# A two-layer attention step on one core: a share of background work at every step, the scale chain issued in pieces, and weights split two jobs ahead

## The chip, the core and the metric

The kernel runs on one core of a Trainium2 chip. The engines are TensorE (PE in the profile, its weight loads PEld), VectorE (DVE), ScalarE (ACT), GpSimd (POOL), and SyncE (SP), from whose queue all the transfers here are issued. The metric is the device time of one execution in microseconds (us), as the median of several runs. Before the change it is 2208.05 us (three runs, 2207.29 to 2210.84).

## The reference

A step of a streaming encoder with two layers, on 2048 prompt frames and 64 sample frames of width 1024. Both layers have the same form and different attention:

```python
def project(x, norm_g, w_in, q_g, k_g, n_heads, n_kv):
    h = rms_norm(x, norm_g)
    p = h @ w_in
    q, k, v, gate = jnp.split(p, [wq, wq + wkv, wq + 2 * wkv], axis=-1)
    q = rms_norm(q.reshape(*lead, n_heads, HEAD_DIM), q_g)
    k = rms_norm(k.reshape(*lead, n_kv, HEAD_DIM), k_g)
...
def gated_attention_layer(...):
    qp, kp, vp, gp = project(x_p, norm_g, w_in, q_g, k_g, n_heads, n_kv)
    op = prompt_band_attention(qp, kp, vp, past_chunks, bias_fn, sinks)
    y_p = x_p + (op * jax.nn.silu(gp)) @ w_out
    ...
```

Layer A has 16 query heads on 2 key heads of 64, a window of the own 64-frame chunk and two before it, a position bias and a sink per head. Layer B has 16 heads with their own keys and values, the own chunk and eight before it, and a bias by clipped distance. The sample frames attend to a cache and to themselves. The outputs are y for both streams and the newest rows of keys and values of both layers. All inputs are float32.

## The kernel before

**Numbers.** Matrix products keep nearly float32 precision by splitting each operand into a high part and a low rest: a projection is three matmuls (high by high, high by low, low by high: lines 679 to 681). In layer B both parts are float16, so the weights are first scaled by a power of two, found on the chip from the largest weight.

**Tiling.** The prompt is cut into eight units of 256 frames (u0 to u7, two tiles of 128 each); the 64 sample frames are a ninth unit. They are worked in the order u0 to u6, sample, u7. Layer A takes four passes of four heads over all units; layer B takes eight passes, each over one pair of heads (`hp` 0 to 7). Between and after them stand the output projections, in blocks of 264 frames.

**Two streams on PE.** Only PE's order is written out by hand. A `Filler` holds all projection jobs of the whole kernel in a list (a job is one unit of one pass) and hands out pieces of them: `filler.to(mark)` steps through generators until so much projection work (counted in us) is done. The attention of layer B (`pipeline` in `layer_b`) goes through the units; a unit has four steps, y = 0 to 3 (two tiles by two heads). Each step issues the score matmuls and the softmax of its tile and head (`scores`), a share of background work, some filler, then what has become due from earlier steps (`due`: the transposes of the probabilities, called `values`, and the products with V), and more filler up to the step's goal. At the end of step 1 the queries and keys of the next unit are transposed (`queries`). For passes after the first, the probabilities of the pair's first head are transposed by DMA instead (`TURNED`), so that two of the four steps have no `values`. In these passes the filler is half a unit ahead of the attention.

**Background work.** Small work on the other engines that isn't bound to a place is put in a queue (`Background`) with a cost in us: head norms (0.6 and 0.4, urgent), gates (0.3), the low parts of queries and keys (`low`, two of 1.0 each, urgent), weight splits (0.66). `bg.share(BL, BP_, KC)` takes from it up to a budget of 1.8 or a quarter of what is queued, whichever is more, and one weight split (two, when more than eight are left). An item issued so comes, on its engine, behind the last softmax instructions issued before it (`anchor`). What isn't taken in time is issued where it is first needed. Within these ties the order on DVE, ACT, POOL and SP is set at build time by a scheduler that goes by the order of issue and by estimates of durations.

**Weights of layer B.** A pass needs eight chunks of 128 x 512 weights, each loaded (line 445), scaled and split into two float16 parts: ACT makes the high part (line 467), DVE the rest (line 470). There are twelve buffers for split chunks (`WN`); a pass holds eight, so four of the next pass can be split early, the others only when the last job of the pass (u7) frees its buffers. `Filler.step` calls for the weights at the start of a job: all of them when the pass begins one job later, and the first four when it begins three jobs later (`EARLY`).

**The scale chain.** `scale_work` runs after each projected tile of layer B, counted by `at` (twice the unit plus the tile). For the next pass it loads the weights once more in chunks (`scan`, line 182), reduces each to its largest value on DVE (line 175, `most`), combines them (`input_top`), turns the column into a row with a PE transpose into the PSUM tile tp and forms a power of two in a few one-element DVE instructions (`input_across`, lines 197 to 208), and spreads it over the partitions with a matmul into tp, a copy to `scl` (lines 212, 213) and a multiplication with the gains, `gsb` (`input_scales`, line 230). The ACT splits read `gsb`. There is one buffer of tp; the transposes of `queries` use it too, and `low` (lines 1367 and 1371) is its last reader. The score matmuls (lines 1416, 1417) and the transposes of probabilities (line 844) share two buffers of the PSUM tile sb, which the softmax pass (line 1420) or the probability splits (lines 816, 817) free.

Of the kernel before, what the change touches and what calls it, by code (L numbers as in the profile page):

```python
# [34 lines left out]
WB = 3  # L35
XB = 4
XN = 7
EARLY = 3
MORE = 4.7
WN = 12  # L40
AVG_A = 5.02
# [7 lines left out]
QY = 1  # L49
# [7 lines left out]
def hybrid_encoder_kernel(  # L57
# [76 lines left out]
    held = {}  # L134
# [85 lines left out]
    def input_across(h):  # L220
        across(h, h + 1)
        e, r, o = row[:, 16:17], row[:, 17:18], row[:, 20:23]
        powers(row[:, h : h + 1], e, r)
        times(o[:, 0:1], r, WB_)
        times(o[:, 1:2], e, 1 / (HB * WB_))
        times(o[:, 2:3], e, 0.5 / VB if h > 0 and len(TURNED) == 2 else 0.5 / (VB * PB))

    def input_scales(h):
        everywhere(h, row[:, 20:23])
        nc.vector.tensor_scalar(gsb[:, h], gain[:, 1, :], S_W(h), 1.0, op0=ALU.mult, op1=ALU.mult)  # L230
# [25 lines left out]
    def scale_work(hp, u, e):  # L256
        at = 2 * u + e
        if hp < 7:
            if at < 8:
                scan(8 * (hp + 1) + at)  # L260
            elif at == 8:
                scan()
                input_top(hp + 1)
            elif at == 10:
                input_across(hp + 1)
            elif at == 11:
                input_scales(hp + 1)
            i = 64 + 3 * hp + (at - 11)
            if 11 <= at < 14 and i < 84:
                scan(i)  # L270
            elif at == 14:
                scan()
        elif u == 0:
            (output_top, output_across)[e]()
        elif at == 2:
            output_scales()
# [585 lines left out]
        return Q2[turn[0] % 2]  # L862


    class Filler:
        def __init__(self):
            self.jobs, self.n, self.gen, self.done, self.total = [], -1, None, 0.0, 0.0
            self.attending = False

        def add(self, prefetch, weights, gen, early=True):  # L870
            j = Item()
            j.prefetch, j.weights, j.gen, j.early = prefetch, weights, gen, early
            self.jobs.append(j)

        def step(self):
            if self.gen is None:
                self.n += 1
                if self.n >= len(self.jobs):
                    return False
                if self.n == 0:  # L880
                    self.x = self.jobs[0].prefetch()
                    self.jobs[0].weights()
                for q in self.x.items:
                    bg.run(q)
                if self.n + 1 < len(self.jobs):
                    nxt = self.jobs[self.n + 1]
                    self.x = nxt.prefetch()
                    if nxt.weights is not None:
                        nxt.weights()
                if self.n + EARLY < len(self.jobs):  # L890
                    nxt = self.jobs[self.n + EARLY]
                    if nxt.weights is not None and nxt.early:
                        nxt.weights(WN - 8)
                self.gen = self.jobs[self.n].gen()
            c = next(self.gen, None)
            if c is None:
                self.gen = None
                return self.step()
            self.done += c
            if not self.attending:  # L900
                bg.drain(FR * c)
            return True
# [5 lines left out]
    filler = Filler()  # L908
    finished = {}

    def layer_a():
# [4 lines left out]
        def add_unit(qd, place, unit):  # L916
            u, T, tiles = unit
# [116 lines left out]
                mine[0].mark = filler.total  # L1034
            if qd == 0 and unit is order[-1]:
                mine[0].mark += 8 * 3 * 256 / 2400
            filler.add(prefetch, weights if place == 0 else None, first if qd == 0 and u == 0 else gen, qd > 1)

        for qd in range(4):
            for place, unit in enumerate(order[2:5] + order[:2] + order[5:] if qd == 1 else order):  # L1040
# [215 lines left out]
    def layer_b():  # L1256
# [4 lines left out]
        def add_unit(hp, unit):  # L1261
            u, T, tiles = unit
            it = Item()
            it.hp, it.unit, it.ready = hp, unit, False
            its.append(it)
            last = u == NU
            cols = slice(2 * hp * HD, (2 * hp + 2) * HD)

            def prefetch():
                for j in range(NO):  # L1270
                    assert finished["x1", j] == 2 or j * OT >= u * UT + T
                rows = None if hp else token_rows(unit)
                st.x[hp, u] = x = load_act(
                    x1, u * UT, T, False, T == TS, None, xs[1], hp > 0, F16, rows
                )
                return x

            def weights(*m):
                if hp not in st.emit:
                    (st.w[hp],), _, st.emit[hp] = load_weights(1, (w_in_b[hp], 512), scale=gsb[:, hp])  # L1280
                st.emit[hp](*m)

            def gen():
                xc = st.x.pop((hp, u))
                it.prs, it.todo = [], []
                it.gate = t("pb", [P, 2, P], 5)
                if "VH" not in held:
                    held["VH"], held["two"] = (
                        x.rearrange("p (a b c) -> p a b c", b=2, c=P)
                        for x in split_at(t("values", [P, 4 * NT * P], 1, F16), 2 * NT * P)  # L1290
                    )
                    held["turn"] = 0
                for e, (tt, t0, n) in enumerate(tiles):
                    out = []
                    c = yield from project((tt, t0, n), xc, st.w[hp], 512, out)
                    if last:
                        pr, sums = evacuate_sample(hp, out[0], it.gate[:, e])
                        it.prs.append(pr)
                        v, kn = pr[:n, 256:384], pr[n:, 0:128]
                        it.todo += [sums] + head_norm(P, pr[:, 0:128]) + gate(P, it.gate[:, e, 0:HD])  # L1300
                        it.todo.append(
                            store_kv(1, slice(n, P), kn, v, kb_s[192:256, cols], vb_s[192:256, cols])
                        )
                        it.ready = True
                        yield c
                        continue
                    pr = evacuate_b(hp, tt, out[0], it.gate[:, e])
                    it.prs.append(pr)
                    v, kn = pr[:n, 256:384], pr[:n, 128:256]
                    it.todo += head_norm(n, pr[:n, 0:256]) + gate(n, it.gate[:n, e])  # L1310
                    if it is its[0] and e == 0:
                        block_scales(TOK - OT)
                    if tt >= NT - 4:
                        o = (tt - (NT - 4)) * P
                        it.todo.append(
                            store_kv(1, slice(0, P), kn, v, kb_p[o : o + P, cols], vb_p[o : o + P, cols])
                        )
                    it.ready = e == len(tiles) - 1
                    scale_work(hp, u, e)
                    yield c  # L1320

            filler.total += 8 * (6 if T == UT else 2) * 512 / 2400
            it.mark = filler.total
            filler.add(prefetch, weights if u == 0 else None, gen)

        for hp in range(8):
            for unit in order:
# [307 lines left out]
        def pipeline():  # L1635
# [12 lines left out]
            def due(at):  # L1648
                flush()
                now = [x for x in todo if x[0] <= at]  # L1650
                todo[:] = [x for x in todo if x[0] > at]
                short, rests, vals = [], [], []
                for _, kind, x in now:
                    if kind == "products":
                        between, rest = products(*x)
                        short += between
                        rests.append(rest)
                    else:
                        {"values": vals, "call": rests}[kind].append(x)
                for x in vals:  # L1660
                    values(*x, short)
                    bg.share(BL, BP_, KC)
                for fn in short + rests:
                    fn()

            for x, it in enumerate(its):
# [13 lines left out]
                for y, (i, h) in enumerate(heads):  # L1680
                    scores(it, i, h)
                    bg.share(BL, BP_, KC)
                    goal(2 * y + 1)
                    due(step)
                    todo += [(step + d, kind, o) for d, kind, o in then(it, i, h)]
                    step += 1
                    if sample and x + 1 < len(its):
                        queries(its[x + 1])
                        flush()
                        near = 1e9  # L1690
                    goal(2 * y + 2)
                    if not sample and y == QY and x + 1 < len(its):
                        queries(its[x + 1])
                        near = 1e9
# [234 lines left out]
```

## Time and profile before

| what | value |
|---|---|
| median of three runs | 2208.05 us (2207.29 to 2210.84) |
| the profiled execution | 2212.35 us, span 2210.5 us |
| PE busy | 2110.9 us, 95% |
| DVE busy | 1547.2 us, 70% |
| ACT busy | 1424.8 us, 64% |
| POOL busy | 999.5 us, 45% |
| mean granted TensorE clock | 0.987 |
| moved by DMA | 372.87 MB, mean 169 GB/s |

The span runs from the first to the last instruction of the profiled execution. Busy times are shares of it by engine; matmuls overlap, so the busy time of PE says how long it had work, not how well it used it. Idle time is told by what ended it: a line "PE sb L1416 <- ACT gt L1237" says that PE's instruction of line 1416, which writes tile sb, waited for ACT's instruction of line 1237, which writes gt. Layer B's attention takes the span from about 880 to 2040 us, the last output projection the rest.

### The profile page before, as it was taken

How to read it: one execution, taken by the hardware profiler on the slowest of the kernel's cores; microseconds unless marked ns; L12 is line 12 of the kernel's file. 1: busy time of each engine (PE TensorE's matmuls, PEld its weight loads, DVE VectorE, ACT ScalarE, POOL GpSimd, SP SyncE). 2: the span in 40 equal slices, each digit the busy share in tenths (PEclk: the TensorE clock that was granted, in tenths of full speed). 3: DMA queues.
4: the chain of work that ended last, by engine and by line, in shares of the span. 5: the costliest groups of instructions: out<-in, count | busy, mean ns of one | idle time of the engine just before them, and what ended most of it. 6: DMA issues, size and time to landing. Idle time of an engine off the chain costs nothing.

```text
span 2210.5 us, 41329 instructions
## 1 busy us (share of the span) xinstructions
PE 2110.9 (95%) x13441; PEld 1526.6 (69%) x13441; DVE 1547.2 (70%) x4105; ACT 1424.8 (64%) x3610; POOL 999.5 (45%) x1509
## 2 busy tenths in 40 slices
PE   7999999999999999999999989999999999998999
PEld 6877888787889997555555555555555555566888
DVE  6769777677676456787777776777767767577542
ACT  6878878677785333666666766766667667576420
POOL 5645544334355355853444444444444445443000
PEclk9999999999999999999999999999999999999999
DMA  8856546856545667445465565664646556345664
GB/s 276 275 160 215 180 125 220 229 164 182 180 128 178 216 192 256 158 143 172 117 180 136 128 178 133 160 167 115 196 118 162 158 118 171 95 105 136 198 202 124
DMA packets 383096, 372.87 MB, mean 169 GB/s; under 512 B 174672, under 2 KB 320352, under 8 KB 382848
## 3 DMA queue, kind: packets, MB, share of 16 engines
q1 hardware_dynamic: 382880, 370.23, 58.0%
q8 instruction: 106, 1.74, 0.3%
q14 instruction: 110, 0.90, 0.1%
HBM read 257.59 MB, written 73.43 MB: 150 GB/s over the span
## 4 chain that ended last, share of the span: by engine, by line
PE 58%; DVE 15%; DMA 9%; ACT 8%; issue 6%; POOL 4%; SPq 1%; POOLq 0%; ACTq 0%; DVEq 0%
PE pj L679 9%; PE pj L681 9%; PE pj L680 9%; PE pj L1772 4%; PE pj L1774 4%; PE pj L1773 4%; DMA scan<-in_w_in_b_dram 3%; DVE p L1420 3%; PE sb L844 2%; PE sa L844 2%; PE o L1607 2%; PE tp L844 2%; PE o L1568 2%; PE sb L1416 1%; ACT p L1429 1%
## 5 line engine op out<-in xcount | busy, mean ns | idle before, releaser
L679 PE MATMUL pj<-wh,xx 128*128 128x512 f16 (+2 forms) x1648 | 644.6, 391 | 5.2 <-ACT pb L702 3.9
L681 PE MATMUL pj<-wh,xx 128*128 128x512 f16 (+2 forms) x1648 | 626.4, 380 | 2.5 <-POOL xx L564 2.5
L680 PE MATMUL pj<-wh,xx 128*128 128x512 f16 x1024 | 392.0, 383 | 0.0
L1429 ACT ACTIVATE p<-p,nm 128x640 f32<-128x640 f32 (+5 forms) x264 | 199.2, 754 | 202.6 <-DVE nm L1420 102.4
L1772 PE MATMUL pj<-xx,wh 128*128 128x264 f32 (+1 forms) x1024 | 291.4, 285 | 8.0 <-DVE res L1778 2.7
L1773 PE MATMUL pj<-xx,wh 128*128 128x264 f32 (+1 forms) x1024 | 288.8, 282 | 0.0
L680 PE MATMUL pj<-wl,xx 128*128 128x512 f32 (+1 forms) x624 | 234.1, 375 | 2.2 <-DVE wl L470 2.2
L1420 DVE CUSTOM_DVE_ANT_0 p<-sb,BT 128x640 f32<-128x640 f32 (+5 forms) x272 | 195.7, 720 | 44.7 <-PE sb L1417 42.3
L564 POOL TENSOR_TENSOR xx<-xraw,xx 128x528 fp32r<-128x528 f32 (+4 forms) x144 | 183.8, 1295 | 88.9 <-ACT xx L563 82.1
L1464 POOL TENSOR_TENSOR values<-p,values 128x640 f16<-128x640 f32 (+2 forms) x112 | 141.2, 1261 | 159.4 <-ACT values L1463 158.8
L1250 POOL TENSOR_TENSOR o<-gt,o 128x256 f32<-128x256 f32 (+1 forms) x132 | 100.8, 763 | 207.7 <-DVE o L1249 96.8
L761 POOL TENSOR_TENSOR f<-f,mhalf 128x4 f32<-128x4 f32 (+2 forms) x187 | 187.5, 1003 | 13.7
L681 PEld LDWEIGHTS <-xx 128*128 128x128 f16 x1024 | 101.0, 99 | 126.4 <-issue 4.7
L756 POOL TENSOR_TENSOR sq<-pa 128x256 f32<-128x256 f32 (+2 forms) x187 | 113.1, 605 | 147.1 <-ACT pa L715 94.3
L1156 ACT ACTIVATE p<-p,nm 128x257 f32<-128x257 f32 (+2 forms) x272 | 134.3, 497 | 51.1 <-DVE nm L1150 42.9
L774 DVE TENSOR_TENSOR pa<-pa,f 128x256 f32<-128x256 f32 (+3 forms) x221 | 120.3, 544 | 57.9 <-POOL f L761 53.2
L679 PEld LDWEIGHTS <-xx 128*128 128x128 f16 x1024 | 101.3, 99 | 71.9 <-issue 3.1
L680 PEld LDWEIGHTS <-xx 128*128 128x128 f16 x1024 | 101.1, 99 | 70.1 <-issue 3.0
L1774 PE MATMUL pj<-xx,wl 128*128 128x264 f32 x512 | 145.7, 285 | 0.8 <-DVE wl L463 0.8
L1774 PE MATMUL pj<-xx,wh 128*128 128x264 f16 x512 | 142.7, 279 | 2.1 <-DVE wh L460 2.1
L1150 DVE CUSTOM_DVE_ANT_0 p<-sa,BT,nsink 128x256 f32<-128x256 f32 (+2 forms) x272 | 117.4, 467 | 36.0 <-PE sa L844 29.9
L679 PEld LDWEIGHTS pj<-wh,xx 128*128 128x128 f32 x624 | 118.7, 190 | 23.0 <-ACT pb L702 4.8
(273 smaller groups left out, 5276.9 us busy)
## 6 DMA issues: line engine op xcount, KB each, us to landing
xx<-xsb SPq DMA_DIRECT2D x112, 512.0 KB, 4.1
xx<-xsa SPq DMA_DIRECT2D x88, 512.0 KB, 4.8
xraw<-oga SPq DMA_DIRECT2D x64, 264.0 KB, 3.6
xraw<-ogb SPq DMA_DIRECT2D x64, 264.0 KB, 3.7
xsa<-xx SPq DMA_DIRECT2D x32, 512.0 KB, 4.1
scan<-in_w_in_b_dram SPq DMA_DIRECT2D x64, 256.0 KB, 4.5
wl<-in_w_in_b_dram SPq DMA_DIRECT2D x64, 256.0 KB, 4.1
xraw<-in_x_dram SPq DMA_DIRECT2D x40, 256.0 KB, 4.0
```

The costliest lines, as they stand in the source:

```text
L564: nc.gpsimd.tensor_tensor(lo, rv, wide(hi), op=ALU.subtract)
L679: nc.tensor.matmul(ps[:n, :C], xh, wh, start=k == 0, stop=False)
L680: nc.tensor.matmul(ps[:n, :C], xh, wl, start=False, stop=False)
L681: nc.tensor.matmul(ps[:n, :C], xl, wh, start=False, stop=k == KC - 1)
L761: nc.gpsimd.tensor_tensor(fv, fv, mhalf[:n, :H], op=ALU.pow)
L1156: ex = nc.scalar.activation(pv[:n, h % 2, : nk + 1], pv[:n, h % 2, : nk + 1], AF.Exp, scale=-1.0, bias=nm[:n, h : h + 1], accum_out=sm[:n, ...
L1420: mi = nc.vector.tensor_tensor_reduce(out=p[r, :nk], in0=S[r, o : o + nk], in1=b, op0=ALU.add, op1=ALU.min, scale=1.0, scalar=3e38, accum_ ...
L1429: ex = nc.scalar.activation(p[:n, :nk], p[:n, :nk], AF.Exp, scale=-1.0, bias=it.nm[:n, c : c + 1], accum_out=it.sm[:n, c : c + 1],)
L1464: lo = nc.gpsimd.tensor_tensor(two[:, :, 1, :], pv, two[:, :, 0, :], op=ALU.subtract)
L1772: nc.tensor.matmul(ps[:, :OT], wh, oh, start=k == 0, stop=False)
L1773: nc.tensor.matmul(ps[:, :OT], wh, ol, start=False, stop=False)
L1774: nc.tensor.matmul(ps[:, :OT], wl, oh, start=False, stop=k == KC - 1)
```

## The change

Three things are changed in layer B.

First, the share of background work in `due` was inside the loop over the `values` of the step; it now comes once in every call of `due` but the first, whether there are values or not.

Second, `input_across` and `input_scales` are no longer issued inside the filler, after tiles at 10 and 11. They are appended to a list, after the tiles at 10 and 12, and the attention takes one from the list at the end of step 3 of a unit that isn't the sample. Whatever is left in the list when the weights of a pass are called for is issued there.

Third, the number of jobs by which the first four weight chunks are split ahead becomes a property of the job: three as before for the passes of layer A that had it and for the output projections, two for layer B.

```diff
-EARLY = 3
...
             elif at == 10:
-                input_across(hp + 1)
-            elif at == 11:
-                input_scales(hp + 1)
+                held["chain"].append(lambda: input_across(hp + 1))
+            elif at == 12:
+                held["chain"].append(lambda: input_scales(hp + 1))
...
+    held["chain"] = []
...
-        def add(self, prefetch, weights, gen, early=True):
+        def add(self, prefetch, weights, gen, early=3):
...
-                if self.n + EARLY < len(self.jobs):
-                    nxt = self.jobs[self.n + EARLY]
-                    if nxt.weights is not None and nxt.early:
+                for nxt in self.jobs[self.n + 2 : self.n + 4]:
+                    if nxt.weights is not None and nxt is self.jobs[min(self.n + nxt.early, len(self.jobs) - 1)]:
                         nxt.weights(WN - 8)
...
-            filler.add(prefetch, weights if place == 0 else None, first if qd == 0 and u == 0 else gen, qd > 1)
+            filler.add(prefetch, weights if place == 0 else None, first if qd == 0 and u == 0 else gen, 3 * (qd > 1))
...
             def weights(*m):
+                while held["chain"]:
+                    held["chain"].pop(0)()
                 if hp not in st.emit:
...
-            filler.add(prefetch, weights if u == 0 else None, gen)
+            filler.add(prefetch, weights if u == 0 else None, gen, 2)
...
                 for x in vals:
                     values(*x, short)
+                if at:
                     bg.share(BL, BP_, KC)
                 for fn in short + rests:
                     fn()
...
                     goal(2 * y + 2)
+                    if not sample and y == QY + 2 and held["chain"]:
+                        held["chain"].pop(0)()
                     if not sample and y == QY and x + 1 < len(its):
```

## The prediction

> **What bounds the kernel now.** I read the page first (busy times), then who waited for whom on PE, then the same for DVE, then the timeline of one head-pair transition of layer B.
>
> ```profile
> span 2210.5 us, 41329 instructions
> PE 2110.9 (95%) x13441; PEld 1526.6 (69%) x13441; DVE 1547.2 (70%) x4105; ACT 1424.8 (64%) x3610; POOL 999.5 (45%) x1509
> ```
>
> PE is busy for all but 99.6 us of the span, so no change that leaves its 13441 matmuls alone can win more than that. This one changes none of them; it can only move the idle time. Layer B's steady part runs from about 1010 to 1990 us. This is everything that PE waited for there:
>
> ```profile
> PE sb L844 <- DVE nm L1420: 13.6, 6, 2.7
> PE tp L197 <- DVE KB L1371: 6.7, 6, 3.8
> PE sb L1416 <- DVE nm L1420: 5.6, 6, 1.9
> PE sb L844 <- ACT p L1429: 5.5, 5, 1.4
> PE sb L844 <- DVE pl L817: 3.7, 8, 0.9
> PE sb L1416 <- ACT gt L1237: 2.9, 3, 1.1
> PE tp L844 <- DVE scl L213: 1.3, 5, 0.3
> PE sb L1416 <- DMA q<-q: 0.4, 1, 0.4
> ```
>
> Columns: total us, times, longest. They sum to 39.7 us. Two kinds are in it. Waits on tile tp (L197, and L844 behind scl) belong to the scale chain: 8.0 us. Waits on tile sb come five or six times each, about once per head pair: 31.3 us. What makes those is seen in one transition. First DVE's own waits in the same stretch, then rows of PE and DVE in order of time (start, us, engine, line; in brackets the idle time before and who ended it).
>
> ```profile
> DVE most L175 <- DMA scan<-in_w_in_b_dram: 40.2, 18, 5.1
> DVE scl L213 <- PE tp L212: 13.2, 6, 6.4
> ...
> 1277.42 0.15 DVE L1425 TENSOR_SCALAR nm<-nm 128x1 f32<-128x1 f32 x1
> 1282.63 0.69 DVE L175 TENSOR_REDUCE most<-scan 128x1 f32<-128x512 f32 x1 [5.07 <-DMA scan<-in_w_in_b_dram]
> 1283.24 0.81 DVE L817 SCALAR_TENSOR_TENSOR pl<-sb,ph 128x640 f16<-128x640 f32 x1
> ```
>
> ```profile
> 1284.67 0.32 PE L1416 MATMUL sb<-KB,q 128*128 128x384 f16 x1 [1.07 <-ACT gt L1237]
> 1292.30 0.77 PE L844 MATMUL sb<-ident,p 128*128 128x128 f32 x5 [1.40 <-ACT p L1429]
> 1294.45 0.32 PE L1416 MATMUL sb<-KA,q 128*128 128x384 f16 x1 [0.74 <-DVE nm L1420]
> 1299.17 0.85 PE L844 MATMUL sb<-ident,p 128*128 128x128 f32 x5 [2.71 <-DVE nm L1420]
> ```
>
> DVE works in order. At 1277.6 the next thing in its queue is the reduction of a scan chunk whose load has not landed; it stands for 5.07 us with the attention's pl (L817) behind it. The gate (gt) waits for pl, the score matmuls for gt: 1.07 us on PE. Then DVE has a backlog, and PE waits 1.40, 0.74 and 2.71 us more. So PE is the bound, and near the sample unit DVE becomes it, because a load blocks it.
>
> **The change, part by part.**
>
> **Chain in pieces.** In the old order `input_across` is issued after u5's first tile and `input_scales` after its second.
>
> ```profile
> 1242.87 0.49 DVE L1371 SCALAR_TENSOR_TENSOR KB<-tp,kf,KB 64x256 f16<-64x256 f32 x1
> ...
> 1243.41 0.27 PE L197 MATMUL tp<-ident,top 128*1 128x128 f32 x1 [0.59 <-DVE KB L1371]
> ...
> 1251.74 0.38 PE L212 MATMUL tp<-scrow,ones 1*128 1x3 f32 x2
> 1252.37 0.66 PE L844 MATMUL tp<-ident,pa 128*128 128x128 f32 x4 [0.25 <-DVE scl L213]
> ...
> 1260.77 0.33 PE L1416 MATMUL sb<-KA,q 128*128 128x384 f16 x1
> ```
>
> The filler is half a unit ahead here: u5's first tile ends with the last step of an attention unit, so the new place of `input_across` (behind the last step's goal) is the old place, 1243.4. Its wait is for the second `low` of the queries, which holds the only tp buffer; with a share at every step that `low` (queued at the end of step 1, together 2.0 of cost beside 1.0 of head norm, against a budget of 1.8) is issued in step 2's `due` instead of step 3's scores, one half-step (2 us) earlier, more than the 0.59 us it was late. `input_scales` moves from 1251.7 to the end of step 3, just ahead of 1260.8, where tp has been free for a whole step and no query transposes stand behind it. Gain: all of the L197 wait but the 3.8 us one, which is `output_across` in the last head pair and isn't touched: 6.7 - 3.8 = 2.9 us. And the 1.3 us behind scl. Sum 4.2 us. The chain's seven small DVE instructions are only moved. The late bound is no gain (another late reader of tp, 0), the other end 8.0.
>
> **Weights two jobs ahead.** Four splits per head pair, each an ACT copy, a DVE subtraction and one 256 KB load issued behind it, move from the job of u6 to that of the sample.
>
> ```profile
> L467 ACT ACTIVATE wh<-wl,gsb x64: 704/712/736, 788.3 to 1863.2; 128x512 f16<-128x512 f32 x64
> L470 DVE SCALAR_TENSOR_TENSOR wh<-wl,gsb,wh x64: 733/751/1817, 789.0 to 1864.0; 128x512 f16<-128x512 f32 x64
> ...
> 1259.79 0.70 ACT L467 ACTIVATE wh<-wl,gsb 128x512 f16<-128x512 f32 x1
> 1270.98 0.38 PE L674 MATMUL pj<-wh,xx 128*128 128x512 f16 x1
> 1292.14 0.72 ACT L467 ACTIVATE wh<-wl,gsb 128x512 f16<-128x512 f32 x1
> ```
>
> The old splits begin at 1259.8 (the other four, bound to buffers that u7's matmuls still read, at 1292.1); the sample's job begins at 1271.0, so the new ones start some 12 us later and fall between 1272 and 1282, one per share. They cost DVE 4 x 0.75 = 3.0 us and ACT 4 x 0.71 = 2.8 us there. The stretches (columns: length; busy us of PE, PEld, DVE, ACT, POOL, instructions in brackets; clock; DMA share; GB/s):
>
> ```profile
> 1259.00:1271.00 12.00, 12.00 (x84) 7.88 (x83) 10.77 (x25) 10.84 (x25) 4.95 (x8) 1.00 0.46 137
> 1271.00:1284.00 13.00, 12.60 (x79) 7.62 (x77) 7.27 (x20) 7.11 (x16) 6.48 (x9) 1.00 0.96 273
> 1284.00:1300.00 16.00, 10.47 (x62) 6.07 (x62) 14.51 (x35) 10.95 (x26) 8.48 (x14) 0.99 0.57 158
> ```
>
> Where they leave (1259 to 1271), PE has no idle time to win. Where they arrive, DVE has 13.00 - 7.27 = 5.7 us free, 5.07 of it the scan's wait, and ACT 5.9. The cover is therefore enough, if the splits come ahead of the scan's reduction in DVE's order. They are issued far earlier in the program than it (it belongs to the next head pair's first job), so I take that: cost nothing. With DVE still busy on them, pl too should no longer be queued behind the reduction, and the 1.07 us before sb<-KB goes (the row with 2.9 in three times). I take -2.9, the rest of the backlog as it is. If they end up behind the reduction, their 3.0 us lengthen the backlog at 1284 to 1300, where DVE is busy 14.51 of 16: up to +3.0 each in six transitions, +18. If the reduction slips behind attention work altogether, the whole group with nm, p and gt goes: 13.6 + 5.6 + 5.5 + 2.9 = -27.6.
>
> The loads have no room: DMA is at 0.96 in 1271 to 1284, and there the scan's chunks are fetched.
>
> ```profile
> 1261.31 0.34 SPq L445 DMA_DIRECT2D wl<-in_w_in_b_dram  x1
> ...
> 1276.90 0.96 SPq L182 DMA_DIRECT2D scan<-in_w_in_b_dram  x2
> ```
>
> Three of four loads (768 KB) move into that stretch on SP's queue; at 273 GB/s they are 2.8 us of transfer. At worst the scan lands that much later and DVE stands 2.8 us longer; at best they stand behind the scan and nothing waits, for they fetch weights of the pair after. I take 0, and keep the bound in the slow case. The transposing DMAs on the same queue have some three steps of slack.
>
> **A share at every step.** From the second head pair on, steps 1 and 2 of a unit had no values and so no second share; now there are eight per unit instead of six. Nothing is added, only issued half a step sooner, ahead of `finish` of the previous unit; its O is needed a unit later. On DVE, gate and `low` may now come before a softmax pass: a bound of one `low` (0.49 us) at places where PE has a spare sb buffer, so I take 0. A second use is at the end of layer B, where the output weights' last splits are late:
>
> ```profile
> PE pj L1774 <- DVE wh L460: 2.1, 2, 1.7
> PE pj L1772 <- ACT wh L459: 1.5, 1, 1.5
> ```
>
> These four splits queue behind four activation splits, one per share. Two more shares per unit issue them sooner, but their buffers come free only with u7's last matmuls. I take half of 3.6: -1.8, ends 0 and -3.6.
>
> **The clock.** After a stretch in which PE was mostly idle, the next 3.4 us run at half clock:
>
> ```profile
> 1296.30:1299.70 3.40, 0.69 (x6) 0.56 (x6) 3.40 (x7) 1.75 (x4) 2.86 (x5) 0.99 0.97 355
> 1299.70:1303.00 3.30, 3.30 (x11) 1.50 (x10) 3.22 (x8) 2.52 (x6) 0.00 (x0) 0.50 0.91 308
> 1576.10:1579.50 3.40, 3.37 (x10) 1.32 (x9) 3.15 (x8) 2.93 (x6) 2.94 (x5) 0.50 0.85 248
> 1722.90:1726.30 3.40, 3.40 (x12) 1.45 (x10) 3.07 (x7) 3.09 (x8) 0.91 (x1) 0.50 0.75 279
> ```
>
> Each costs 1.7 us; three are in transitions. I leave them where they are; with the backlog they would go too (-5.1), and each transition made worse may add one. [...]
>
> **Sum.** -4.2 - 2.9 - 1.8 = -8.9 us. The profiled execution took 2212.35 us (span 2210.5 and 1.85 around it), so 2203.4; the median of the runs shown is 2208.05, 4.3 below it, so 2199 in its terms.
>
> **Rivals.**
>
> *The backlog goes too.* The splits push the scan's reduction past its landing, and DVE never blocks. For it: DVE's 5.7 us of room and 3.0 us of new work with an earlier claim. Against: the other scan waits (40.2 us in 18) aren't near the splits, and the four late splits still fall from 1292 on. With all of it: -4.2 - 27.6 - 1.8 - 5.1 = -38.7, so 2169; half of it 2188.
>
> *Slower: the early splits meet the blocked DVE.* One mechanism: the splits (or pl behind them) land behind a scan that is itself later by its share of 2.8 us, in the one stretch where DVE is the bound. For it: DMA 0.96, DVE 14.51 of 16 just after, and the old place was free of PE waits. Price up to 3.0 + 2.8 a transition; it decides once a transition loses more than 8.9 / 6 = 1.5 us. With 3.0 each, and three more half-clock stretches (5.1): +18 + 5.1 - 4.2 - 1.8 = +17, so 2225; with 2 each 2214.
>
> *No difference.* The shares change little, since the queue was emptied anyway; tp's wait goes but the order on DVE shifts by as much elsewhere. 2204 to 2212.
>
> **How the numbers follow.** A measurement here tells about 0.2% (4.4 us) from no change. Forecast (2193 to 2203.6) 0.40; backlog gone (below 2193) 0.16; no difference (2203.6 to 2212.5) 0.18; slower 0.26. Faster 0.56. The range cuts half of the slow case's tail and the far end of the fast one: 2181 to 2220. The forecast's own range is 2193 to 2206, from its terms' ends (2.9 of pl and 3.6 of the tail kept or lost).
>
> **What would show it.** Right: no wait of L197 on KB L1371 in the first seven head pairs, none of tp L844 on scl; L212 half a unit later; four wh splits of each pair between the sample's first matmul and 12 us after; the sb<-KB wait on gt gone; the longest scan wait in a transition well under 5 us. Wrong: scan waits longer than 5.07, more waits of sb on nm L1420 than 13.6 us in six, or more 0.50 stretches; or, for the better, none of these. What would make it wrong is DVE's order, which is fixed at build time from estimates of durations and may shift anywhere in layer B.

## The result and the profile after

The changed kernel takes 2229.53 us (median of six runs, 2227.33 to 2233.45) against 2211.48 us for the kernel before on the same chip (six runs, 2207.29 to 2213.34). The ratio is 1.0087, with a 95% interval of 1.0073 to 1.0101: slower by 0.9%, some 18 us. (The ratios are worked out from all runs and needn't be those of the medians.) The forecast was 2199, faster by 0.4%. Sign and size are wrong, and the time lies above the range.

The profiled execution of the changed kernel took 2233.45 us. First its page, span and busy times.

```profile
span 2231.6 us, 41342 instructions
PE 2117.9 (95%) x13441; PEld 1526.6 (68%) x13441; DVE 1543.3 (69%) x4105; ACT 1430.2 (64%) x3610; POOL 998.6 (45%) x1509
```

The span is 21.1 us longer than before (2231.6 - 2210.5). PE's idle time grew from 99.6 to 2231.6 - 2117.9 = 113.7 us and its busy time by 7.0 us, with the same 13441 matmuls; DVE, ACT and POOL run as many instructions as before, with busy times within 5.4 us of those. Next what PE waited for in layer B's steady part, 1010 to 1990 us (columns: total us, times, longest).

```profile
PE sb L1418 <- DVE nm L1422: 10.9, 19, 1.1
PE o L843 <- POOL o L1535: 6.8, 6, 1.2
PE sb L843 <- ACT values L718: 6.0, 3, 2.0
PE sb L843 <- DVE nm L1422: 5.2, 5, 1.0
PE sb L843 <- DVE pl L816: 5.0, 9, 0.7
PE sb L843 <- POOL G L1450: 4.3, 4, 1.1
PE sb L843 <- ACT pa L714: 3.8, 2, 2.0
PE tp L196 <- DVE KB L1373: 3.6, 1, 3.6
```

(Line numbers shifted by the edit: the scores are L1418 and L1419, the softmax pass L1422, the transposes L843, the second `low` L1373, the scan's reduction L174. Of the tiles, nm holds the row extremes that the softmax pass writes, p the probabilities, ph and pl their two parts, G the gate times the reciprocal of the softmax sums, gt the same transposed, and o the attention's output.) Three readings. The wait of tp on KB is down from six to one, as forecast. The wait of 2.7 us of sb on nm at a transition is gone, but each of the six transitions still has one of 1.9 to 2.4 us, now on ACT's `values` or pa or, once, on DVE's sm, and in four of them 1.1 us on POOL's G come right behind it. And in place of six waits of the scores on nm there are 19, and six on POOL's o are new. Paired one by one with the matmuls of the kernel before (their order differs in few places), those of the changed kernel fall back by 20.3 us between 1010 and 2040 us: about 7 at the sample's outputs, about 9 in the 10 us ahead of the transitions' long waits, about 5 in the units between, while the long waits themselves balance out. So the loss is spread over each pass; it isn't a longer backlog at the transition, as the prediction's slow case had it. DVE's own waits for two releasers, in the same stretch, the kernel after first and then the kernel before (whose row on the scan the prediction shows):

```profile
DVE sm L1439 <- ACT p L1431: 33.0, 40, 1.1
DVE most L174 <- DMA scan<-in_w_in_b_dram: 23.0, 14, 3.4
```

```profile
DVE sm L1437 <- ACT p L1429: 8.5, 14, 1.0
```

The scan blocks DVE for 23.0 us instead of 40.2. But DVE now stands 40 times, 33.0 us, in front of `sm`, the reciprocal of the softmax sums, waiting for the exponential on ACT. Before, there were 14 such places. This row turned out to be the one to follow.

### The profile page after: what moved, and what is told of

Same layout as the page of the kernel before. It is cut to its first block, busy times and chain, and to the rows that moved or that the text cites. A ratio compares the mean times of both kernels' runs of the same rounds, so it can differ in the third digit from the quotient of the medians.

```text
span 2231.6 us, 41342 instructions
## 1 busy us (share of the span) xinstructions
PE 2117.9 (95%) x13441; PEld 1526.6 (68%) x13441; DVE 1543.3 (69%) x4105; ACT 1430.2 (64%) x3610; POOL 998.6 (45%) x1509
## 4 chain that ended last, share of the span: by engine, by line
PE 56%; DVE 17%; DMA 9%; ACT 8%; issue 5%; POOL 4%; SPq 1%; POOLq 0%; ACTq 0%; DVEq 0%
PE pj L678 9%; PE pj L680 9%; PE pj L679 9%; PE pj L1777 4%; PE pj L1779 4%; PE pj L1778 4%; DVE p L1422 3%; DMA scan<-in_w_in_b_dram 3%; PE sb L843 2%; PE sa L843 2%; DMA xraw<-in_x_rows_dram 2%; ACT p L1431 2%; DVE pl L816 2%; PE tp L843 2%; PE o L1609 2%
## 5 line engine op out<-in xcount | busy, mean ns | idle before, releaser
L1422 DVE CUSTOM_DVE_ANT_0 p<-sb,BT 128x640 f32<-128x640 f32 (+5 forms) x272 | 195.8, 720 | 57.2 <-PE sb L1419 54.1
```

The costliest lines, as they stand in the source:

```text
L1422: mi = nc.vector.tensor_tensor_reduce(out=p[r, :nk], in0=S[r, o : o + nk], in1=b, op0=ALU.add, op1=ALU.min, scale=1.0, scalar=3e38, accum_ ...
```

## The experiments

The theory at the start: the share at every step costs the time, since it puts `low`, gate and splits in front of a softmax pass. The rival: the splits two jobs ahead cost it, as the prediction's slower case had it. Each of the three parts was run alone or left out; then the share was cut down.

**The share alone.** Only this edit, in the kernel before:

```diff
                 for x in vals:
                     values(*x, short)
+                if at:
                     bg.share(BL, BP_, KC)
```

> Only the first of the three edits: the share in due comes once at every step. Theory 'placement' (the cost is that four weight splits per pass now meet the sample's stretch): -2 to +3 us against before, six or so waits of about 0.6 us on tp gone, the first score waits of the transition as before. Theory 'share' (background work issued ahead of what is due in the same step delays it): +8 to +14 us, and PE's wait of tile o on POOL's o (about 1.2 us once per pass, 6.8 us in all in the changed kernel) is here.

Measured: 2235.81 against 2213.88 us, ratio 1.0094 (1.0071 to 1.0117). It is the whole loss, and more than the +8 to +14 us that the theory of the share gave. To see how, one step of one unit (the fourth, y = 3), first in the kernel before, from its timeline (start, us, engine, line, tiles; in brackets the idle time before and its releaser):

```profile
1539.16 0.27 PE L1417 MATMUL sb<-KB,q 128*128 128x256 f16 x1
1539.46 0.82 DVE L1420 CUSTOM_DVE_ANT_0 p<-sb,BT 128x640 f32<-128x640 f32 x1 [0.21 <-PE sb L1417]
1540.33 0.49 DVE L1367 SCALAR_TENSOR_TENSOR q<-tp,qf,q 64x256 f16<-64x256 f32 x1
1540.83 0.49 DVE L1371 SCALAR_TENSOR_TENSOR KB<-tp,kf,KB 64x256 f16<-64x256 f32 x1
1541.35 0.18 DVE L1437 RECIPROCAL sm<-sm 128x4 f32<-128x4 f32 x1
```

The scores end at 1539.16 + 0.27 = 1539.43, and the softmax pass starts 0.03 us later: DVE had waited for it. Then ACT forms the exponential, and in that time DVE does the two parts of the second `low`. They end at 1541.32, and `sm` follows at 1541.35, 1.07 us after the end of the pass. In the listing below it follows 1.06 us after the pass with no `low` between, so the `low` cost nothing here. Now the same step with the share at every step:

```profile
1556.53 0.49 DVE L1367 SCALAR_TENSOR_TENSOR q<-tp,qf,q 64x256 f16<-64x256 f32 x1
1557.03 0.49 DVE L1371 SCALAR_TENSOR_TENSOR KB<-tp,kf,KB 64x256 f16<-64x256 f32 x1
1557.55 0.29 DVE L783 SCALAR_TENSOR_TENSOR pb<-sq,pb 128x128 f32<-128x128 f32 x1
...
1558.04 0.27 PE L1417 MATMUL sb<-KB,q 128*128 128x256 f16 x1
1558.09 0.75 DVE L470 SCALAR_TENSOR_TENSOR wh<-wl,gsb,wh 128x512 f16<-128x512 f32 x1
1558.87 0.85 DVE L1249 TENSOR_TENSOR o<-o,o 64x256 f32<-64x256 f32 x2
1559.75 0.82 DVE L1420 CUSTOM_DVE_ANT_0 p<-sb,BT 128x640 f32<-128x640 f32 x1
1561.63 0.18 DVE L1437 RECIPROCAL sm<-sm 128x4 f32<-128x4 f32 x1 [1.05 <-ACT p L1429]
...
1563.92 0.77 PE L844 MATMUL sb<-ident,p 128*128 128x128 f32 x5 [0.63 <-DVE pl L817]
```

(Rows of both engines, put in order of time.) The `low`, a piece of the head norm (`pb`) and a weight split are issued in step 2, so they are tied only behind step 2's softmax, and stand in front of step 3's. (The merging of o stands ahead of the pass in the kernel before too, at 1538.40; there it was done before the scores were.) The scores end at 1558.31, the softmax pass starts at 1559.75: 1.44 us late instead of 0.03. And the time behind it that the `low` had filled is now 1.05 us of idle DVE. The work moved out of the exponential's shadow (the time that DVE waits for ACT anyway), where it was free. PE's waits of this kernel (1010 to 1990):

```profile
PE sb L1416 <- DVE nm L1420: 14.7, 20, 2.5
PE sb L844 <- DVE pl L817: 8.3, 14, 0.7
PE o L844 <- POOL o L1533: 6.8, 6, 1.2
PE sb L844 <- ACT p L1429: 5.1, 5, 1.4
PE sb L844 <- POOL G L1448: 4.4, 5, 1.3
PE tp L197 <- DVE KB L1371: 3.6, 1, 3.6
```

The waits of the scores, the six on POOL's o and those on G, which the changed kernel has too, are here: they come with the share. So does the shorter wait of tp on KB.

**The weights alone, and weights with chain.** The first has the earlier splits, the second that and the chain in pieces, both with the share as it was before (the edit is the change's own diff without the other parts).

> Only the third edit: the first four weight chunks of a pass of layer B are split two jobs ahead instead of three; chain and shares as before. Theory 'placement': +8 to +14 us, the two waits of tile sb of about 1.0 us each at the start of the unit before the sample's (2.4 us per pass) and a half-clock stretch in nearly every transition. Theory 'share': -3 to +3 us; the longest scan wait in a transition falls from 5.1 to under 2 us and no new wait comes.

> The changed kernel without its first edit (shares as before; chain in pieces and weights two jobs ahead). Theory 'placement': +6 to +12 us, as with the weights alone less the 4 us of waits on tp. Theory 'share': -8 to 0 us, the gain that I had forecast.

Measured: the weights alone 0.999 (0.9979 to 1.0001), not told apart from no change; weights and chain 0.9985 (0.9972 to 0.9997), faster by 0.15%, 3 to 4 us. These two parts don't cost anything; the prediction's slower rival falls. Of what the theory of the share said of the weights alone, the time came in, but not the rest: the longest scan wait fell to 3.3 us, not under 2, and PE now waits for the splits (2.7 us on DVE's, 1.3 on ACT's). The second kernel's waits on PE and the scan's on DVE:

```profile
PE sb L843 <- DVE nm L1422: 20.6, 10, 2.7
PE tp L196 <- DVE KB L1373: 6.7, 6, 3.8
PE pj L679 <- DVE wh L469: 2.7, 2, 1.6
```

```profile
DVE most L174 <- DMA scan<-in_w_in_b_dram: 20.0, 14, 3.3
```

The scan's wait is halved (40.2 to 20.0), and the waits of sb on gt and of tp on scl are gone; those of the scores on nm are down from 5.6 to 1.7 us. But ten long waits of the transposes on nm (20.6 us) stand where six did (13.6), and the splits themselves are late three times (1.3 us more on ACT's). All of PE's waits that the profile lists in this stretch add up to 39.5 us, against 39.7 before: what DVE won at the scan doesn't show there. And the chain in pieces leaves tp's wait on KB as it was: that one goes with step 2's share.

**The change without the chain edit.**

> The changed kernel without its second edit (the chain issued inside the filler, as before). Both theories: within 5 us of the changed kernel (+18 us against before), since the chain's waits are worth 4 us at most. If the chain's new place is itself a cost, this is faster than the changed kernel by more than 5 us.

Measured: 2229.91 against 2213.88 us, 1.008 (1.006 to 1.0101), as with the chain edit (1.0087, 1.0073 to 1.0101). The chain is worth about nothing beside the share.

**What in the share costs.** Four cuts of it, each in the kernel before, with the old share kept where a step has values. The first puts the extra share behind the step's products instead of ahead of them:

```diff
                 for fn in short + rests:
                     fn()
+                if at and not vals:
+                    bg.share(BL, BP_, KC)
```

> The kernel before with the extra share in the steps without values, but issued behind the step's calls and products instead of ahead of them. The share alone cost +21 us. Theory 'ahead of the due work': all of it was that the background work stands ahead of what is due, so within 4 us of before. Theory 'ahead of the softmax' (the second low and the gate now stand ahead of step 3's softmax pass on DVE, and the scores, the sums and G of that step come late): only the sample's wait of tile o (7.6 us over the passes) goes, +11 to +16 us.

The second lets the extra share take no weight splits:

```diff
+                if at and not vals:
+                    bg.drain(max(BL, bg.cost / BP_), 0)
                 for fn in short + rests:
```

> The extra share ahead of the calls, but it may not take weight splits. Theory 'weights' (splits crowd into fewer steps): within 4 us of before. Theory 'ahead of the softmax': +16 to +21 us, as with the whole share; at most the transitions get better.

Measured: 1.0093 (1.0075 to 1.0112) behind the products, so the place within the step doesn't matter. That is some 20 us, above what either theory gave, and the wait on POOL's o, which was to go, stays (6.7 us in 6). Without splits 1.0055 (1.0036 to 1.0075), some 12 us, between the two forecasts: the splits are some 0.4% of the 0.94. PE's waits of the second still hold the new one:

```profile
PE o L844 <- POOL o L1533: 7.2, 6, 1.4
```

The third lets the extra share pass over the `low` parts (the only items of cost 1.0); the fourth gives it in step 1 only, before the `low` is queued.

```diff
-        def drain(self, budget, most=KC):
+        def drain(self, budget, most=KC, skip=False):
...
+                if skip and it.cost == 1.0:
+                    continue
...
+                if at and not vals:
+                    bg.share(BL, BP_, KC, True)
```

> The extra share ahead of the calls, but it passes over the low parts of queries and keys (cost 1.0); gates, head norms and weights may go. Theory 'ahead of the softmax', by the low parts: -3 to +6 us, the waits of sb on nm and of the G transposes as before. Theory 'weights': +15 to +21 us. If the gate alone is enough to delay step 3: +6 to +15 us.

```diff
-            def due(at):
+            def due(at, y=0):
...
+                if y == 1 and not vals:
+                    bg.share(BL, BP_, KC)
...
-                    due(step)
+                    due(step, y)
```

> The extra share only in step 1 of a unit, where neither low parts nor the new tile's head norm are queued yet; not in step 2. Theory 'ahead of the softmax': -4 to +3 us, since only weights and what is left over can move. Theory 'weights': about half of the loss, +8 to +14 us.

Measured: without `low` 1.0035 (1.0021 to 1.0049); in step 1 only 0.9985 (0.9968 to 1.0002). So the whole loss comes with step 2's share. Some 0.59% of it is `low` (0.94 - 0.35), some 0.39% the splits (0.94 - 0.55), which make about the whole. These are differences of ratios, each uncertain by some 0.3%, and they take it that the two add up: no run leaves out both, and a share that passes over `low` has budget left for other items, so gates and head norms may have a part. The 0.35% that stays without `low`, some 8 us, is more than the theory of the `low` parts gave (-3 to +6) and in the range of the gate's. Waits of the kernel without `low` on PE, then on DVE:

```profile
PE sb L1418 <- DVE nm L1422: 15.2, 12, 2.4
PE tp L197 <- DVE KB L1373: 6.6, 6, 3.6
PE sb L846 <- POOL G L1450: 5.0, 5, 1.3
```

```profile
DVE sm L1439 <- ACT p L1431: 11.1, 18, 1.0
```

With `low` back in its place, the wait on POOL's o is gone, that of tp on KB is back at 6.6, and DVE's idle time in front of `sm` is 11.1 us in 18. The waits of the scores on nm and of the transposes on G stay, though the theory said that they would be as before. (The profiled execution of this kernel is the fastest of its 12, 2212.58 against a median of 2220.66 us, and that without splits the slowest of its 8, 2237.27 against 2226.47: their waits can't be set against their losses.) DVE's idle time in front of `sm` parts all the kernels here in two groups: 7 to 11 us in 12 to 18 where `low` stays behind step 3's softmax, and 33 to 39 us in 40 to 47 in the five where step 2's share can take it (the change, the share alone, with early weights, behind the products, without splits). It tells where `low` stands, and not the loss: 35.2 us go with 0.55%, 38.0 with 0.94, and 11.1 still with 0.35.

| kernel | ratio to before | DVE: sm waits for ACT's p, us (times) |
|---|---|---|
| before | 1 | 8.5 (14) |
| after | 1.0087 | 33.0 (40) |
| share alone | 1.0094 | 38.0 (46) |
| share and weights | 1.008 | 34.4 (41) |
| share behind products | 1.0093 | 39.1 (47) |
| share without splits | 1.0055 | 35.2 (43) |
| share without `low` | 1.0035 | 11.1 (18) |
| share in step 1 only | 0.9985 | 7.1 (12) |
| weights alone | 0.999 | 11.0 (18) |
| weights and chain | 0.9985 | 10.7 (18) |

**Is there a version that beats both?** First the parts that don't hurt: weights, chain and the share in step 1 only.

> The changed kernel with its extra share in step 1 of a unit only: chain in pieces, weights two jobs ahead, and no new share in step 2, where the low parts and the gate are queued. Theory 'ahead of the softmax': the changed kernel's loss is gone, -8 to -2 us against before (the two harmless parts gave -0.1 to -0.15% each). If the parts hurt one another: +2 us or more.

Then the block of DVE by the scan itself, which the prediction put behind each transition's waits. In the kernel before, the reduction is tied behind the last softmax instruction issued on DVE, as the background items are, so that the scheduler can't put it ahead of attention work:

```diff
-            nc.vector.tensor_reduce(
+            r = nc.vector.tensor_reduce(
                 most[:, j : j + 1], raw, axis=AX.X, op=ALU.max, apply_absolute_value=True
             )
+            if bg.lazy and r.ins.engine in bg.anchors:
+                behind(r.ins, bg.anchors[r.ins.engine])
```

> The kernel before with one tie more: in layer B the reduction of a scan chunk on DVE may not stand ahead of the last softmax instruction issued before it, so that DVE no longer reaches it before its load has landed. Theory 'blocked DVE' (DVE's wait for the scan, 40 us in 18 times, makes the waits on tile sb at each transition, 27.6 us in all): DVE's scan waits fall under 15 us and the time by 8 to 20 us. If the transitions' waits come from the splits and the sample's own work: -3 to +3 us.

And both together:

> The two before together. Theory 'blocked DVE': -10 to -25 us against before. Otherwise as the first of them, -8 to 0 us.

Measured: 0.998 (0.9966 to 0.9994), 0.992 (0.9898 to 0.9943) and 0.9944 (0.9925 to 0.9963); medians 2197.99, 2185.67 and 2191.66 us against 2202.51. The tie of the scan alone is the fastest, some 17 us below the kernel before. Its longest waits on PE (1010 to 1990):

```profile
PE sb L846 <- DVE nm L1422: 11.1, 6, 2.2
PE tp L199 <- DVE KB L1373: 5.0, 6, 3.8
PE sb L846 <- DVE pl L819: 3.7, 5, 1.7
PE sb L1418 <- DVE nm L1422: 2.8, 5, 0.6
```

DVE's list of this kernel has no scan wait of the 40.2 us left, and the waits of sb on gt are gone. Of the group of waits that the prediction put at 27.6 us (sb on nm, p and gt), 14.3 are left: 11.1 and 2.8 on nm, as shown, and 0.4 on p. With the parts of the change added it is no better: the median is 6 us higher, and the intervals overlap. What the parts won alone isn't there a second time. Once the scan doesn't block, the early splits have no block to win back, which would explain it; that is argued, not shown.

## Why the prediction was wrong

**The step that failed** is in the part on the share: "a bound of one `low` (0.49 us) at places where PE has a spare sb buffer, so I take 0". Three things in it were wrong.

- *The size.* It isn't one half of a `low` (0.49 us is one of its two instructions) that moves in front of the pass but both (0.98 us), with head norm and a split behind them: the pass of the step shown is 1.44 us late.
- *The cover.* The work was named as free where it goes to, and not looked for where it came from. It came from behind the pass, where DVE waits for the exponential anyway: a timeline of step 3 in the kernel before shows `low` fitting that gap exactly. With the change DVE stands 24.5 us longer in such gaps (33.0 - 8.5). These are not the microseconds of the loss, as the table shows, but they tell that the work has left its place.
- *The spare buffer.* A pass that starts late in step 3 delays exponential, sums, G and the transposes, and the scores of the next unit. PE's order is the same in the two traces (share alone and before), so the matmuls can be paired one by one. Between 1010 and 2040 us the kernel with the share falls 23.9 us further back: 13.3 us at the scores with KA, 10.5 at the transposes with G, 7.6 at the sample's transposes, which wait for POOL's o (6 places of about 1.3), less 4.0 at the chain's transposes, 3.2 at the scores with KB and 3.7 in the output projection; all others add 3.4. At the transitions the waits on G come largely in place of those on nm just before them. The spare buffer doesn't cover these waits.

The range followed from this zero: it had no case in which the share cost anything, though the prediction itself named the place and the engine.

**The chain** (forecast 4.2). The 2.9 us of tp's wait on KB did go, in the change and with the share alone; without the share it stayed (6.7, 6). So "that `low` is issued in step 2's `due`, one half-step earlier" was right and is the very move that cost the 0.59%: the prediction counted its gain, 2.9 us, and not its price. The wait on scl (1.3 us) went with the pieces.

**Weights two jobs ahead** (cost 0, gain 2.9). Right in kind: the splits cost nothing, the scan's wait shrank by half, the sb wait on gt went. Right in size only roughly: weights and chain gained 3 to 4 us where 2.9 + 1.3 = 4.2 stand without the share. That this is near is in part luck, for the rows moved otherwise: the splits are late by 2.7 and 1.3 us, and the transposes' wait on nm grew from 13.6 to 20.6, while that of the scores and that on p shrank. The slower rival had the size (2225), but with the wrong mechanism: its parts, run without the share, are not slower.

**The tail** (forecast 1.8). The waits on wh in the output projection, 3.6 us, went entirely, but only with the share (that in step 1 alone is enough). In the last unit the share put a wait of 3.3 us on POOL's G in their place, so nothing is left of it.

**The backlog and the rival that it goes.** The tie of the scan bears the mechanism out in part: without the block, 17 us are won, where the prediction gave 27.6 for the whole group of waits and 5.1 for the clock. About half of the group went (27.6 to 14.3), and the lost clock, summed as below, fell from 15.0 to 8.2 us. But five transitions keep a wait of 2.19 us on nm with no scan wait left, so the block isn't what makes those. And no part of the change brings it about: the early splits only halve the block.

**Two readings that don't hold.** The prediction took PE's 99.6 us of idle time for the most that can be won with the same 13441 matmuls. PE's busy time isn't fixed by them: in the profiled executions it is 2100.0 us with the scan tied and 2124.4 with the share alone, against 2110.9 before, in part by the clock: in the kernel before, the 128x512 projection matmuls start 0.43 us apart at half clock and 0.22 at full. And its own range for the forecast, 2193 to 2206, doesn't come out of the two terms that it names: with 2.9 and 1.8 lost it ends at 2203.9, and 2193 needs the chain's 8.0 as well.

**The clock** (forecast unchanged). The changed kernel has a stretch at half clock in each of six transitions, but the lost clock from 1000 us to the end (the time at half clock, times one half) is 17.1 us against 15.0 before: 2.1 us of the 21.1. With the share alone it is 22.4, so 7.4 of the 27.3 us between the two profiled spans. Still it is no main cause of the loss: the two runs of the share alone with the highest clock, 0.993 and 0.990, took 2226.17 and 2227.53 us, and the slowest of the 23 runs of the kernel before beside them 2220.09 at 0.987. About 4.6 us more of the difference between the profiled executions lie before 300 us, in layer A, where both kernels have the same instructions in the same order: that belongs to the two executions.

## What to carry to other kernels

Before moving small work on an engine that isn't the bound, look up where it stands now: here, in the shadow of another engine's latency (ACT's exponential), it cost nothing (`sm` 1.07 us after the softmax pass with a `low` between, 1.06 without), and the same work half a step sooner, in front of the instruction that starts that latency, delayed that instruction by 1.44 us and left the shadow empty. Price the place it leaves and not only the place it arrives at; the row to watch is the engine's own wait on that latency (here 8.5 us before, 33.0 after). And a reduction fed by a transfer, put into DVE's order ahead of its landing, blocked what stood behind it here (40.2 us in 18 times, up to 5.1 at once): tie it behind urgent work before moving anything else around it.

## What was not expected of the hardware

A granted clock of one half came after stretches in which PE was busy for far longer than the 0.69 of 3.40 us that the prediction shows ahead of one. Two transitions of the changed kernel, each with the stretch before and the one at half clock (columns as in the prediction), and PE's timeline in the first:

```profile
1591.00:1594.40 3.40, 1.77 (x10) 1.12 (x11) 3.40 (x9) 1.30 (x4) 1.94 (x4) 0.99 1.03 349
1594.40:1597.80 3.40, 3.40 (x11) 1.32 (x9) 2.79 (x6) 2.40 (x7) 1.90 (x3) 0.50 0.80 284
1734.30:1737.70 3.40, 1.23 (x7) 0.82 (x8) 3.40 (x10) 1.33 (x4) 2.26 (x4) 1.00 0.94 306
1737.70:1741.10 3.40, 3.40 (x11) 1.34 (x10) 2.77 (x6) 2.94 (x7) 1.44 (x2) 0.50 1.01 380
```

```profile
1591.53 0.74 PE L843 MATMUL sb<-ident,p 128*128 128x128 f32 x5 [2.01 <-ACT values L718]
1593.34 0.69 PE L843 MATMUL sb<-ident,G 128*128 128x128 f32 x2 [1.08 <-POOL G L1450]
```

In the first, PE was busy for 1.77 of 3.40 us, and no single gap was longer than 2.01 us. So a gap as long as the 2.71 us ahead of the prediction's first half-clock stretch isn't needed for it: here shorter ones came together (2.01 and 1.08 us). And shorter waits at more places (the change took the 2.71 us gap away) didn't save the clock (17.1 us lost against 15.0). In each of the traces before and after, the starts of all half-clock stretches lie on one grid of 3.413 us, to within 0.004 us. Cut at that grid, the two traces tell this much (from 10 us on, pieces of 3.413 us at full clock): all 18 pieces with PE busy for under 1.42 us were followed by one at half clock, 9 of the 18 with 1.42 to 1.81 us, and one of the 1220 with more. In the first transition shown the piece, 1590.95 to 1594.36, has 1.73 us, 1.39 of it transposes, and no gap over 1.08 us. What decides between 1.42 and 1.81 us, no run here shows.
